# Pages by the time they are free, a searched order with GpSimd's rows behind accumulating DMAs, and f and g by seven from chunk 2 on

## The chip, the core and the metric

The kernel runs on one core of one Trainium2 chip. Its time is the device time of one execution in microseconds; the figure for a kernel is the median of its runs. A profiled execution also has a span, from the first to the last instruction that the profile shows.

The engines have short names in the profile: PE is TensorE (matmuls), PEld its weight loads, DVE is VectorE, ACT ScalarE, POOL GpSimd, SP the engine that issues most DMAs. Every instruction stands under the same line, L288, because one helper records and emits them all, so the text goes by the names of tiles.

## What is computed

One layer with a gated short convolution. `x` is 1024 x 1024 in float32, the inner width is 2048:

```python
def short_conv_mixer(u, w_in, conv_w, w_out):
    z, bg, cg, v = jnp.split(u @ w_in.astype(u.dtype), 4, axis=-1)
    y = bg * causal_dwconv(cg * v, conv_w) * jax.nn.silu(z)
    return y @ w_out.astype(u.dtype)

u = rms_norm(h, pre_norm[i])
m = short_conv_mixer(u, sc_w_in[j], sc_conv_w[j], sc_w_out[j])
h = h + rms_norm(m, post_norm[i])
```

## The kernel before

**Arithmetic.** Each float32 operand is split in a high and a low part, and each product is three matmuls (low x high, high x low, high x high). The input projection runs over 16 chunks `c` of 128 channels, each with two pairs `p = 2c` (the blocks CG and V) and `p = 2c + 1` (Z and BG). A pair is a 2 x 2 block product that is done with seven products, a to g, instead of eight; each is 12 matmuls of 512 columns. Some of the seven are themselves done by seven again, over a whole chunk: `by_seven(z, c)` (line 794) says so for z = b, f or g, from chunk DEEP, DEEP_F or DEEP_G on to the limits in LAST (b to chunk 15, f to 14, g to 13). A plain product costs 2 x 12 matmuls of 512 columns a chunk, one by seven 7 x 6 matmuls of 256 columns (`deep_product`, line 1432).

**What a product by seven needs.** Once for each z: `deep_subs` (line 1362) forms differences of the pages of u on GpSimd, eight rows of 256 columns, and `deep_split` (line 1375) splits four parts c', d', e', g' in high and low; with `by_bank` that is two casts and two copies to PSUM on ScalarE and one subtraction on VectorE for each part. g's source is read back from DRAM first (`load_ug`, line 1678). The table `UNDER` (line 1688) says after which product of which pair each of these is recorded. In each chunk besides: `deep_sums` (line 1399, four rows on GpSimd) and `deep_prep` (line 1414, the split of the weights), with `split_by_bank` (line 805) for several weights where f goes by seven.

**The output projection's weights.** They are summed in DRAM while the chunks run: `sums_plan` (line 979) and `out_sums` (line 995) issue plain copies into `t_d` on SP and then 16 accumulating DMAs on GpSimd's queue; `fetch_t` and `add_t` (lines 950 and 957) form other sums by loads, four GpSimd rows a time, and stores; `TODO` (line 1644) says at which pair. The stage after the chunks reads `t_d` in the order c, e, d, g (the tiles ru_c, ru_e, ru_d, ru_g).

**The order of the work.** From `plan.record()` on nothing is issued at once: each operation becomes an `Op` with a duration and its needs. `Plan.deadlines` (line 371) gives each a latest time, `boost` in PLAN moves single ones by hand-written amounts (by number of the operation), and `Plan.arrange` (line 424) runs the operations through a small model of the engines, which picks on each engine the ready one that is due first. TensorE's operations keep their order. The model knows that VectorE rows on SBUF operands and GpSimd rows take turns (`lock`, `own`, `grant`, `turn`). `take` (line 501) gives a GpSimd row to an idle VectorE. `sum_at` keeps accumulating DMAs apart. `emit` (line 631) then issues everything in that order, engine by engine.

**Pages.** Most SBUF tiles are pages of 512 floats a partition, 32 of them, made by `page` (line 691) under one tag `pg` with 32 buffers. `arrange` counts how many are free; which buffer a tile gets is left to the pool.

Of the kernel before, what the change touches and what calls it, by code (L numbers as in the profile page):

```python
# [18 lines left out]
PAGES = 32  # L19
DEEP = 2  # L20
DEEP_F = 3
DEEP_G = 4
LEAD = 7.0
PLAN = {
# [3 lines left out]
    "turns": 1,  # L28
    "hard": 2.0,
# [173 lines left out]

class Tile(View):

    __slots__ = ("pool", "args", "kw", "made", "parts", "writes", "reads", "left", "space", "key", "read", "summed", "n")

    def __init__(self, pool, shape, dtype, kw):
        ids = np.arange(int(np.prod(shape[1:]))).reshape(1, *shape[1:])
# [1892 lines left out]
```

## Time and profile before

| | |
|---|---|
| median of 3 runs | 776.25 us (776.20 to 776.41) |
| profiled execution | 776.59 us |
| its span | 774.8 us |
| mean granted TensorE clock | 0.998 |

The page gives the busy time of each engine in the span, then the chain of work that ended last. The views that the prediction quotes: waits (who waited for whom: us in total, times, longest), the timeline (start, length, engine, operation, tiles out<-in, shape, count, and in brackets the idle time before it and what ended it), groups of instructions (count, busy us, mean ns, idle before), and windows (stretch, length, then busy us and count of PE, PEld, DVE, ACT and POOL, the clock, the DMA share and GB/s).

### The profile page before, as it was taken

How to read it: one execution, taken by the hardware profiler on the slowest of the kernel's cores; microseconds unless marked ns; L12 is line 12 of the kernel's file. 1: busy time of each engine (PE TensorE's matmuls, PEld its weight loads, DVE VectorE, ACT ScalarE, POOL GpSimd, SP SyncE). 2: the span in 40 equal slices, each digit the busy share in tenths (PEclk: the TensorE clock that was granted, in tenths of full speed). 3: DMA queues.
4: the chain of work that ended last, by engine and by line, in shares of the span. 5: the costliest groups of instructions: out<-in, count | busy, mean ns of one | idle time of the engine just before them, and what ended most of it. 6: DMA issues, size and time to landing. Idle time of an engine off the chain costs nothing.

```text
span 774.8 us, 12631 instructions
## 1 busy us (share of the span) xinstructions
PE 763.8 (99%) x4266; PEld 668.0 (86%) x4266; DVE 669.9 (86%) x1009; ACT 451.2 (58%) x861; POOL 442.6 (57%) x397
## 2 busy tenths in 40 slices
PE   8999999999999999999999999999999999999996
PEld 7888888888988898988888888888888889889885
DVE  6899878786989898999899989797899899977993
ACT  7774456675755565756565656556553656564831
POOL 2518994558695859777788687565637100600321
PEclk9999999999999999999999999999999999999999
DMA  9222432354747575556667673724254998666842
GB/s 315 67 55 55 122 111 80 121 161 146 177 136 171 170 161 146 165 143 191 197 177 212 176 203 94 185 81 140 84 163 131 359 388 278 202 224 212 266 142 108
DMA packets 117136, 130.09 MB, mean 168 GB/s; under 512 B 7320, under 2 KB 74704, under 8 KB 116944
## 3 DMA queue, kind: packets, MB, share of 16 engines
q1 hardware_dynamic: 112560, 120.77, 48.4%
q0 software_dynamic: 4352, 8.39, 7.3%
q8 instruction: 33, 0.54, 0.3%
q14 instruction: 31, 0.25, 0.1%
q10 hardware_dynamic: 160, 0.14, 0.0%
HBM read 101.74 MB, written 44.30 MB: 188 GB/s over the span
## 4 chain that ended last, share of the span: by engine, by line
PE 97%; DVE 1%; issue 1%; DMA 1%; ACT 0%; POOL 0%; DVEq 0%; POOLq 0%; ACTq 0%
PE px L288 40%; PE pv L288 15%; PE po_x L288 11%; PE px2b L288 5%; PE px2f L288 3%; PE po_v L288 3%; PE pp L288 3%; PE px2g L288 3%; PE pv2b L288 2%; PE pv2f L288 2%; PE pf_x L288 1%; PE pb_x L288 1%; PE py2b L288 1%; PE py L288 1%; PE pv2g L288 1%
## 5 line engine op out<-in xcount | busy, mean ns | idle before, releaser
L288 PE MATMUL px<-u_d,wdh 128*128 128x512 f32 x248 | 76.7, 390 | 0.0
L288 PE MATMUL px<-u_a,wah 128*128 128x512 f32 x248 | 76.7, 390 | 0.0
L288 PE MATMUL pv<-u_e,weh 128*128 128x512 f32 x248 | 76.6, 390 | 0.0
L288 PE MATMUL px<-u_c,wch 128*128 128x512 f32 x248 | 76.6, 390 | 0.0
L288 ACT COPY beside<-raw 128x512 f32<-128x512 f32 x64 | 37.9, 592 | 37.5 <-DVE wal L288 13.3
L288 PEld LDWEIGHTS px<-u_d,wdh 128*128 128x128 f32 x248 | 46.6, 188 | 9.1
L288 PEld LDWEIGHTS px<-u_c,wch 128*128 128x128 f32 x248 | 46.7, 188 | 9.1
L288 PEld LDWEIGHTS pv<-u_e,weh 128*128 128x128 f32 x248 | 46.6, 188 | 9.0
L288 PEld LDWEIGHTS px<-u_a,wah 128*128 128x128 f32 x248 | 46.7, 188 | 8.9
L288 ACT COPY sna<-px 128x512 f32<-128x512 f32 x30 | 17.6, 586 | 60.4 <-PE px L288 55.6
L288 DVE SCALAR_TENSOR_TENSOR cv<-gpad,cw,cv 128x1024 f32<-128x1024 f32 x32 | 49.4, 1544 | 2.5 <-ACT cv L288 2.3
L288 PE MATMUL px<-u_d,wdl 128*128 128x512 f32 x124 | 48.8, 393 | 0.7 <-DVE wdl L288 0.7
L288 PE MATMUL px<-u_a,wal 128*128 128x512 f32 x124 | 48.6, 392 | 0.0
L288 PE MATMUL px<-u_c,wcl 128*128 128x512 f32 x124 | 48.5, 391 | 0.0
L288 PE MATMUL pv<-u_e,wel 128*128 128x512 f32 x124 | 48.5, 391 | 0.0
L288 POOL TENSOR_TENSOR sf<-raw,sc 128x512 f32<-128x512 f32 x27 | 41.2, 1524 | 10.8 <-issue 5.5
L288 POOL TENSOR_TENSOR raw<-raw,raw 128x512 f32<-128x512 f32 x31 | 45.2, 1459 | 3.5 <-DVE se L288 2.9
L288 POOL TENSOR_TENSOR sc<-se,raw 128x512 f32<-128x512 f32 x24 | 37.3, 1555 | 15.2 <-PE px L288 4.9
L288 POOL TENSOR_TENSOR se<-raw,raw 128x512 f32<-128x512 f32 x22 | 31.1, 1414 | 23.6 <-DVE sna L288 4.7
L288 POOL TENSOR_TENSOR rs_post<-ve_post,minus_half 128x1 f32<-128x1 f32 x7 | 4.9, 704 | 64.5 <-DVE ve_post L288 64.5
L288 ACT COPY snc<-px 128x512 f32<-128x512 f32 x31 | 18.0, 580 | 26.5 <-PE px L288 26.5
L288 POOL TENSOR_TENSOR sne<-snc,sne 128x512 f32<-128x512 f32 x10 | 13.5, 1346 | 33.7 <-ACT snc L288 31.9
(491 smaller groups left out, 2618.2 us busy)
## 6 DMA issues: line engine op xcount, KB each, us to landing
raw<-in_sc_w_in SPq DMA_DIRECT2D x128, 256.0 KB, 3.8
y_d<-cv SPq DMA_DIRECT2D x16, 512.0 KB, 2.7
s_d<-s SPq DMA_DIRECT2D x32, 256.0 KB, 3.2
t_d<-in_sc_w_out POOLq DMA_DIRECT2D x16, 512.0 KB, 7.9
t_d<-in_sc_w_out SPq DMA_DIRECT2D x16, 256.0 KB, 5.2
tb<-in_sc_w_out SPq DMA_DIRECT2D x16, 256.0 KB, 4.0
t_d<-t_d SPq DMA_DIRECT2D x16, 256.0 KB, 4.7
s<-y_d SPq DMA_DIRECT2D x16, 256.0 KB, 3.1
```

The costliest lines, as they stand in the source:

```text
L288: getattr(engine, name)(*(self.plain(a) for a in args), **{k: self.plain(a) for k, a in kw.items()})
```

## The change

Three things, and the numbers that go with them.

1. Pages are handed out by the run-through. `arrange` keeps a list of free page numbers; a new page takes the first, a page whose last use is over goes to the end. A tile then has its own tag, `pg` and the number, with one buffer. The tiles made before the recording take their numbers from a list, HEAD_SLOTS.
2. The run-through has a flag `kept`: after an accumulating DMA GpSimd keeps its turn on the shared operands as long as its next row is one of that sort, also ahead of a waiting VectorE row. Accumulating DMAs are kept apart by 11.0 instead of 15.0. The table of amounts in `boost` is another one, with 308 entries in place of 695.
3. DEEP_F goes from 3 to 2 and DEEP_G from 4 to 2: f goes by seven in chunk 2 too, g in chunks 2 and 3. UNDER is rewritten to suit. TODO follows DEEP_F, so `fetch_t` and `add_t` come two pairs earlier. The sums into t_d come in the order e, c, d, g from pair 15 on (e, d, c, g from pair 10 before), still 16 accumulating DMAs.

```diff
-DEEP_F = 3
-DEEP_G = 4
+DEEP_F = 2
+DEEP_G = 2
+HEAD_SLOTS = (
+    0, 23, 31, 30, 29, 28, 27, 26, 25, 24, 22, 21, 20, 1, 19, 18, 2, 17, 16, 15, 14, 3, 13, 12, 11, 10, 4, 7, 9, 8,
+    5, 6, 31, 29, 30, 28, 23, 0, 10, 11, 27, 26, 7, 4, 29, 15, 31, 16, 13, 3, 21, 22, 1, 20, 26, 27, 25, 30, 4, 7,
+)
...
+    "apart": 11.0,
...
     def get(self):
         if self.made is None:
-            self.made = self.pool.pool.tile(list(self.args[0]), self.args[1], **self.kw)
+            kw = self.kw
+            if kw["tag"] == "pg":
+                kw = dict(kw, tag=f"pg{self.slot}", bufs=1)
+            self.made = self.pool.pool.tile(list(self.args[0]), self.args[1], **kw)
...
+        held = [t.slot for k, ts in self.taken.items() if k[1] == "pg" for t in ts if t in self.users]
+        slots = self.slots = [n for n in range(PAGES) if n not in held]
...
-            if e == "vector" and not late and nxt is not None and nxt.lock:
+            more = nxt is not None and nxt.lock
+            self.kept = self.kept and (e == "vector" or more)
+            if more and (not late if e == "vector" else self.kept):
                 own[1] = e
...
+                        if x.key[1] == "pg":
+                            x.slot = slots.pop(0)
...
                     if e == "gpsimd" and op.order:
-                        self.sum_at = t + 15.0
+                        self.kept = True
+                        self.sum_at = t + p["apart"]
...
                     if left_of[x] == 0 and (x.read or x.key[1] == "cv"):
                         free[x.key] += 1
+                        if x.key[1] == "pg":
+                            slots.append(x.slot)
...
-    sums_plan(2 * DEEP_F + 4)
+    sums_plan({(n, h): 15 + 4 * "ecdg".index(n) + 2 * h for n in "ecdg" for h in (0, 1)})
...
-        ("d", 2 * DEEP): lambda: (deep_split("b", "c'", True), deep_split("b", "e'", True)),
-        ("f", 2 * DEEP): lambda: deep_subs("f", [0, 1]),
-        ("g", 2 * DEEP): lambda: deep_split("b", "d'", True),
-        ("e", 2 * DEEP + 1): lambda: deep_split("b", "g'", True),
-        ("d", 2 * DEEP_F): lambda: deep_split("f", "c'", True),
-        ("a", 2 * DEEP_F + 1): lambda: deep_split("f", "e'", True),
-        ("g", 2 * DEEP_F): lambda: deep_split("f", "d'", True),
-        ("c", 2 * DEEP_F + 1): lambda: deep_split("f", "g'", True),
-        ("e", 2 * DEEP_G - 2): load_ug,
-        ("e", 2 * DEEP_G - 1): lambda: deep_subs("g", [0]),
-        ("a", 2 * DEEP_G): lambda: deep_subs("g", [1]),
-        ("a", 2 * DEEP_G + 1): lambda: deep_split("g", "c'", True),
-        ("c", 2 * DEEP_G + 1): lambda: deep_split("g", "e'", True),
-        ("e", 2 * DEEP_G + 1): lambda: deep_split("g", "g'", True),
-        ("d", 2 * DEEP_G + 1): lambda: deep_split("g", "d'", True),
+        ("c", 2 * DEEP): lambda: (deep_split("b", "c'", True), deep_split("b", "e'", True)),
+        ("e", 2 * DEEP): lambda: (deep_split("b", "d'", True), deep_subs("f", [0, 1])),
+        ("d", 2 * DEEP): load_ug,
+        ("a", 2 * DEEP + 1): lambda: [deep_split("f", i, True) for i in ("c'", "e'", "d'")],
+        ("c", 2 * DEEP + 1): lambda: (deep_split("b", "g'", True), deep_split("f", "g'", True)),
+        ("e", 2 * DEEP + 1): lambda: deep_subs("g", [0, 1]),
+        ("d", 2 * DEEP + 1): lambda: [deep_split("g", i, True) for i in ("c'", "e'", "g'", "d'")],
```

More of the change, by code (lines that the diff above doesn't have):

```diff
@@ L204 @@
 class Tile(View):
-    __slots__ = ("pool", "args", "kw", "made", "parts", "writes", "reads", "left", "space", "key", "read", "summed", "n")
+    __slots__ = ("pool", "args", "kw", "made", "parts", "writes", "reads", "left", "space", "key", "read", "summed", "n", "slot")
     def __init__(self, pool, shape, dtype, kw):
@@ L215, in __init__ @@
         self.n = pool.plan.made
+        self.slot = None
     def get(self):
         if self.made is None:
-            self.made = self.pool.pool.tile(list(self.args[0]), self.args[1], **self.kw)
+            kw = self.kw
+            if kw["tag"] == "pg":
+                kw = dict(kw, tag=f"pg{self.slot}", bufs=1)
+            self.made = self.pool.pool.tile(list(self.args[0]), self.args[1], **kw)
         return self.made
@@ L231, in tile @@
         if not self.plan.recording:
+            if kw["tag"] == "pg":
+                t.slot = self.plan.slots.pop(0)
             t.get()
@@ L256, in __init__ @@
         self.nc, self.recording, self.ops, self.room, self.taken, self.made = nc, False, [], {}, {}, 0
+        self.slots = list(HEAD_SLOTS)
         for name in ("tensor", "vector", "scalar", "gpsimd", "sync"):
@@ L554, in arrange @@
                 note(held, ("held", op.engine, op, False))
-        self.shift, self.sum_at = 0.0, t
+        self.shift, self.sum_at, self.kept = 0.0, t, False
         self.stalls = []
@@ L570, in arrange @@
                     order.append(op)
-                    for x in op.news:
+                    for x in sorted(op.news, key=lambda x: x.n):
                         made.add(x)
                         free[x.key] -= 1
+                        if x.key[1] == "pg":
+                            x.slot = slots.pop(0)
                         owed[x.key].remove(op)
@@ L624, in arrange @@
                         note(ops[o].soft, None)
-                for x in op.tiles:
+                for x in sorted(op.tiles, key=lambda x: x.n):
                     left_of[x] -= 1
@@ L977, with sums_plan @@
     SUM_AT = {}
-    def sums_plan(p0):
-        order = [(n, h) for n in "edcg" for h in (0, 1)]
-        for j, (n, h) in enumerate(order):
+    def sums_plan(at):
+        for (n, h), p in at.items():
             js = slice(h * CQ, (h + 1) * CQ)
@@ L989, in sums_plan @@
             for b in range(CQ):
-                SUM_AT.setdefault(p0 + 2 * j - 1, []).append((to[n][:, b : b + 1], src[:, b : b + 1], False))
+                SUM_AT.setdefault(max(p - 1, 2), []).append((to[n][:, b : b + 1], src[:, b : b + 1], False))
             for k in (0, 1):
                 ks = slice(k * CQ // 2, (k + 1) * CQ // 2)
-                SUM_AT.setdefault(p0 + 2 * j + k, []).append((to[n][:, ks], more[:, ks], True))
+                SUM_AT.setdefault(p + k, []).append((to[n][:, ks], more[:, ks], True))
     def out_sums(p):
```

124 rows, old and new, of the table PLAN are left out of this document.

## The prediction

> **What bounds the kernel now.** I read the page first (its totals and chain), then the wait view of TensorE, then TensorE's own timeline around the waits that it names, and last the busy time of the other engines chunk by chunk.
>
> ```profile
> span 774.8 us, 12631 instructions
> PE 763.8 (99%) x4266; PEld 668.0 (86%) x4266; DVE 669.9 (86%) x1009; ACT 451.2 (58%) x861; POOL 442.6 (57%) x397
> PE 97%; DVE 1%; issue 1%; DMA 1%; ACT 0%; POOL 0%; DVEq 0%; POOLq 0%; ACTq 0%
> ```
> ```profile
> PE pw L288 <- DVE idle L288: 1.1, 1, 1.1
> PE pv2f L288 <- DVE dwf2l L288: 0.9, 1, 0.9
> PE px L288 <- DVE wdl L288: 0.7, 1, 0.7
> PE pk L288 <- DVE ve_pre L288: 0.6, 1, 0.6
> ```
>
> 97% of the chain that ends last is matmuls. The wait view of TensorE has six lines and 4.1 us in all; those on pw, pk and pp belong to the opening, in program order ahead of the recorded plan, and the diff leaves that order alone. So only two things can get shorter: the matmuls themselves, and the two waits on pv2f and px. No line of that view names a DMA: the loads are early enough.
>
> **Term 1, fewer matmul columns.** A product by seven takes 7 x 6 = 42 matmuls of 256 columns a chunk, a plain one 24 of 512. The change turns f of chunk 2 and g of chunks 2 and 3 into products by seven: three chunk-products. The price stands in the trace already, as the distance from the first matmul of product c in one chunk to the first in the next. Chunk 2 has only b by seven, chunk 3 b and f, chunk 6 all three:
>
> ```profile
> 100.01 0.39 PE L288 MATMUL px<-u_c,wcl 128*128 128x512 f32 x1
> 137.74 0.39 PE L288 MATMUL px<-u_c,wcl 128*128 128x512 f32 x1
> 175.07 0.39 PE L288 MATMUL px<-u_c,wcl 128*128 128x512 f32 x1
> 249.58 0.40 PE L288 MATMUL px<-u_c,wcl 128*128 128x512 f32 x1
> 286.50 0.40 PE L288 MATMUL px<-u_c,wcl 128*128 128x512 f32 x1
> ```
>
> 37.73 us, 37.33 us and 36.92 us: f by seven saves 0.40, g by seven 0.41. Three of them: 0.40 + 2 x 0.41 = **1.2 us less**. (Two of g's sub-products slide behind the next chunk's product c; they come back at g's other end.) This term hides behind nothing, since TensorE is the path.
>
> The Trainium skill, "TensorE: Matmul & The Clock Gate", section "Phases on the wall clock", gives the back-to-back gap as N/2.4 + 2.5 ns, 216 ns for 512 columns and so, as an estimate, 109 ns for 256; three chunk-products would then save 1.8 us, and the sum would be 0.6 us lower. The chunk lengths above say 0.40 and 0.41 for one, so the trace does not agree, and the sum goes by the trace.
>
> **Term 2, the two waits in chunk 5.** Here is TensorE at both, then VectorE and GpSimd in the microseconds before:
>
> ```profile
> 234.59 0.40 PE L288 MATMUL pv2b<-u_b,dwb2h 128*128 128x256 f32 x2
> 235.89 0.39 PE L288 MATMUL pv2f<-u_f,dwf2l 128*128 128x256 f32 x1 [0.90 <-DVE dwf2l L288]
> ...
> 237.87 0.28 PE L288 MATMUL px2f<-ufdl_deep,dwf2h 128*128 128x256 f32 x1
> 237.99 0.28 PE L288 MATMUL px2f<-ufdh_deep,dwf2h 128*128 128x256 f32 x1
> 239.00 0.50 PE L288 MATMUL px<-u_d,wdl 128*128 128x512 f32 x1 [0.74 <-DVE wdl L288]
> ```
> ```profile
> 231.99 3.25 DVE L288 TENSOR_TENSOR dwb<-raw,dwb 128x256 fp32r<-128x256 f32 x1
> 235.16 0.68 DVE L288 TENSOR_TENSOR dwf2l<-beside,dwf2h 128x512 fp32r<-128x512 f32 x1
> ```
> ```profile
> 230.41 1.15 POOL L288 DMA_DIRECT2D t_d<-in_sc_w_out  x1
> 231.16 1.17 POOL L288 TENSOR_TENSOR dsg<-dsg,raw 128x256 f32<-128x256 f32 x1
> 231.87 1.15 POOL L288 TENSOR_TENSOR dsg<-raw,raw 128x256 f32<-128x256 f32 x1
> 232.57 1.14 POOL L288 TENSOR_TENSOR dsg<-raw,dsg 128x256 f32<-128x256 f32 x1
> 233.56 1.38 POOL L288 TENSOR_TENSOR se<-raw,raw 128x512 f32<-128x512 f32 x1
> ```
>
> Matmuls of 256 columns start every 0.12 us here (237.87 to 237.99), so 1.06 us were lost at 235.89 and 0.89 at 239.00: 1.95 us, of which the wait view counts 1.64 since modelled ends overlap. The cause is in the rows below: GpSimd issues an accumulating DMA and then runs four rows back to back, and a VectorE subtraction with two SBUF inputs, queued at 231.99, ends only at 235.24, after 3.25 us. The order of before had no such rule: its run-through lets VectorE in between two GpSimd rows. The new run-through has it (the flag `kept`: GpSimd keeps its turn from the DMA on while its next row is of that kind), so it will put something harmless there. **1.95 us less**, at most; nothing, if the wait turns up elsewhere.
>
> The Trainium skill, "SBUF — State Buffer", section "Who interferes with whom", says that of a VectorE op with two SBUF inputs and a GpSimd op the second to issue blocks until the first finishes. By it the subtraction would have waited for one row and ended near 233.4 (an estimate), with no wait on TensorE; the 3.25 us over four rows differ, so the measurement decides.
>
> **Term 3, what the change adds.** The one-off work for products by seven (deep_subs, deep_split) was spread over chunks 1 to 5 and now falls in chunk 2. Busy time of chunks 1, 2, 3 and 6 (columns: PE, PEld, DVE, ACT, POOL, clock, DMA share, GB/s):
>
> ```profile
> 64.60:100.00 35.40, 35.40 (x157) 29.29 (x157) 31.60 (x32) 16.05 (x28) 32.90 (x23) 1.00 0.30 88
> 100.00:137.70 37.70, 37.70 (x187) 32.01 (x186) 28.40 (x42) 23.23 (x49) 26.63 (x22) 1.00 0.25 79
> 137.70:175.10 37.40, 37.40 (x206) 32.54 (x206) 28.62 (x47) 25.76 (x53) 20.12 (x20) 1.00 0.48 148
> 249.60:286.50 36.90, 36.90 (x224) 32.97 (x223) 33.15 (x50) 21.24 (x41) 27.65 (x25) 1.00 0.63 162
> ```
> ```profile
> L288 DVE TENSOR_TENSOR ugcl_deep<-beside,ugch_deep 128x512 fp32r<-128x512 f32 x1 | 0.7, 692 | 0.2 <-ACT beside L288 0.2
> L288 ACT COPY beside<-deepg 128x256 f32<-128x256 f32 x8 | 3.0, 376 | 1.2 <-DVE wdl L288 0.8 <-DVE dwb1l L288 0.3
> L288 ACT CAST uggh_deep<-deepg 128x256 fp32r<-128x256 f32 x2 | 0.8, 406 | 0.0
> L288 POOL TENSOR_TENSOR deepg<-deepg 128x256 f32<-128x256 f32 x4 | 2.9, 740 | 0.0
> L288 POOL TENSOR_TENSOR t<-t,tb 128x256 f32<-128x256 f32 x8 | 8.6, 1074 | 0.0
> ```
>
> One split is two casts and two copies on ScalarE (2 x 0.41 + 2 x 0.38 = 1.6 us) and one subtraction on VectorE (0.69). Twelve of them (b, f and g, four each) on top of a chunk like the sixth give VectorE 33.15 + 12 x 0.69 = 41.4 us and ScalarE 21.24 + 12 x 1.6 = 40.4 us in a chunk of 36.9. GpSimd has 27.65, less two accumulating DMAs (1.15 each) and four add_t rows (1.07 each in the last row) that chunk 2 hasn't, plus 16 rows of deep_subs at 0.74 for f and g: 33.2. So VectorE is 4.5 us over and ScalarE 3.5, **if nothing slides out**. It can slide: VectorE has 3.8 us free in chunk 1, and chunk 3, which loses its own f splits, has 37 - 33 = 4; ScalarE has 19 free in chunk 1. Deadlines limit the sliding: b's first splits are due in chunk 2, g's last two just after the first product of chunk 3. The price is therefore between 0 and 4.5 us, and where part of VectorE's time is waiting for GpSimd (the 3.25 us row is 0.41 of work), less than it looks.
>
> The accumulating DMAs stay 16, and move:
>
> ```profile
> L288 POOL DMA_DIRECT2D t_d<-in_sc_w_out x16: 1153/1171/1328, 189.0 to 485.0; - x16
> L288 SPq DMA_DIRECT2D ru_c<-t_d x8: 319/320/778, 626.4 to 635.2; - x8
> L288 SPq DMA_DIRECT2D ru_g<-t_d x8: 319/320/382, 707.6 to 729.5; - x8
> ```
>
> From pairs 10 to 25 they go to 15 to 30, five pairs of some 18.5 us: the last near 578 to 605. In the new order e, c, d, g the sum c is done by pair 22 (near 430, read at 626) and g by pair 30, read at 707, so nobody comes to wait for them. The add_t loads go two pairs earlier, load_ug (four loads on SP) to chunk 2, where the DMA share is 0.25. In chunks 7 to 10 add_t and sums coincide, before in 5 to 11: no loss visible, a small gain possible, both costed at 0.
>
> Pages: a tile now gets the page that has been free longest by the run-through, as a tag of one buffer, and its writer waits for that page's last reader. Behind a waiting fetch on SP stand the stores of cv and s and the copies into t_d, on ScalarE and VectorE the next splits. Before, SP already waits like that, and TensorE doesn't notice:
>
> ```profile
> SPq L288 <- ACT beside L288: 29.4, 8, 9.3
> ```
>
> Fetches lead by two pairs (37 us) and that longest wait is 9.3 us, so I take 0; a loss needs a page freed late on the chip where the plan has none to spare, and I bound it by the largest wait of TensorE now, 1.1 us, a gain by the 1.64 that are counted in term 2.
>
> What do I take for term 3? Between 0 and 4.5 I take 0.9, the nearest row that there is: the smaller of the two waits by which the old order missed the chip.
>
> **Sum.** The profiled execution took 776.59 us, 1.79 more than its span and 0.34 more than the median of 776.25. 776.59 - 1.2 - 1.95 + 0.9 = 774.3, and by the median **774.0 us**. A measurement tells 0.2% from no change, 1.55 us: faster is under 774.7, slower over 777.8.
>
> **Rivals.**
> - *The wait moves* (0.28): 16 accumulating DMAs still each hold VectorE back, and the packed chunk 2 costs one or two waits like those of before. Then only term 1 is left: 776.25 - 1.2 = 775.0, up to 777 where chunk 2 adds 2. For it: the DMAs are not fewer. Against: 15 of the 16 cost TensorE nothing already now.
> - *Chunk 2 saturates* (0.20, the other side): ScalarE and VectorE can't slide, g's and f's splits come late, TensorE waits on them between 120 and 145 us. It decides once more than 4.7 us of waits are left (1.2 + 1.95 + 1.55). Price: 4.5 from VectorE's sum and 0.9 elsewhere: 776.25 - 3.15 + 5.4 = 778.5. For it: both engines are over 36.9 by the sum. Against: 7.8 us free on VectorE on both sides.
> - *The run-through doesn't do what it says* is inside the first: if GpSimd's run of rows had another cause than the DMA, the 1.95 stay, 775.0.
> - *Nothing is left over* (part of the forecast): 776.25 - 3.15 = 773.1.
>
> **How the numbers follow.** Forecast 0.52: 773.1 to 774.7, likeliest 774.0. The range must reach into both rivals: 772.9 to 778.0 leaves out half of the saturated case and a little at the bottom. Faster 0.52, same 0.28, slower 0.20.
>
> **What would show it.** Right: 126 matmuls of 256 columns more and 72 of 512 fewer, 4320 in all; the distance between first matmuls of product c 36.9 us from chunk 3 on; no wait on dwf2l or wdl after an accumulating DMA, GpSimd's run of rows falling on VectorE rows that read PSUM. Wrong in term 3: lines in TensorE's wait view on ubgl, ufdl, ugcl, dwf or dwg between 120 and 145 us. Wrong in the pages: a wait on a DMA into raw, or a weight's cast waiting for a page's old reader. The forecast falls if those waits exceed 1.7 us together.

## The result and the profile after

The changed kernel takes 773.27 us (median of 6 runs, 772.79 to 774.06) against 776.37 us for the kernel before beside it: 3.1 us less, a ratio of 0.996 with a 95% interval of 0.9947 to 0.9972. The profiled execution took 772.83 us, its span is 771.0 us. The forecast was 774.0 us, faster.

The page's totals and chain, then the whole wait view of TensorE (who waited for whom: us in total, times, longest), both of the changed kernel, where the helper's line is L252:

```profile
span 771.0 us, 12816 instructions
PE 762.2 (99%) x4320; PEld 669.6 (87%) x4320; DVE 673.9 (87%) x1022; ACT 458.8 (60%) x880; POOL 462.2 (60%) x416
PE 98%; DVE 1%; DMA 0%; ACT 0%; POOL 0%; issue 0%; POOLq 0%; ACTq 0%
```
```profile
PE pw L252 <- DVE idle L252: 1.1, 1, 1.1
PE pp L252 <- ACT u_a L252: 0.5, 1, 0.5
PE pk L252 <- DVE xa L252: 0.3, 1, 0.3
```

The program has 4320 matmuls instead of 4266, as counted ahead. The lines on pv2f and px are gone and none came in their place: what is left of waits is the opening. Next, TensorE's timeline at the first matmul of product c in pairs 4, 6, 8, 12 and 14, the starts of chunks 2, 3, 4, 6 and 7:

```profile
99.55 0.39 PE L252 MATMUL px<-u_c,wcl 128*128 128x512 f32 x1
135.02 0.40 PE L252 MATMUL px<-u_c,wcl 128*128 128x512 f32 x1
171.94 0.40 PE L252 MATMUL px<-u_c,wcl 128*128 128x512 f32 x1
245.78 0.40 PE L252 MATMUL px<-u_c,wcl 128*128 128x512 f32 x1
282.70 0.40 PE L252 MATMUL px<-u_c,wcl 128*128 128x512 f32 x1
```

Chunk 3 now takes 36.92 us, as chunk 6 does. Chunk 2 takes 35.47, because two of g's sub-products slide behind the next product c, 1.4 us that the other end pays back.

To place the 3.1 us, one row of the view by tile is enough. It gives the first and the last start of the low part of product c, pair 1 to pair 31. First the kernel before, then the changed one:

```profile
L288 PE MATMUL px<-u_c,wcl x124: 389/389/396, 45.6 to 605.0; 128*128 128x512 f32 x124
```
```profile
L252 PE MATMUL px<-u_c,wcl x124: 389/389/396, 45.2 to 601.2; 128*128 128x512 f32 x124
```

This middle took 559.4 us and takes 556.0: **3.35 us less** by the starts to the nanosecond. All of it lies in chunks 2 to 5: from the first matmul of product c in chunk 2 to that in chunk 6 the kernel before took 149.57 us (100.01 to 249.58, shown in the prediction) and the changed one 146.23 (99.55 to 245.78). The opening ended 0.46 us earlier in this profile, and the stretch from the last such matmul to the end is the same within 0.02 us. The 0.46 can't be put down to the change: in the eleven profiles of this study the opening ends between 45.15 and 45.61 us, and two profiles of the changed kernel alone differ by 0.24.

One row more, of the accumulating DMAs in the changed kernel (first and last start):

```profile
L252 POOL DMA_DIRECT2D t_d<-in_sc_w_out x16: 1145/1176/1332, 276.2 to 556.7; - x16
```

The first of them now starts at 276.2 us instead of 189.0. So in chunk 5, where both waits were, there is no accumulating DMA any more.

### The profile page after: what moved, and what is told of

It reads as the page before. It is cut to its first block, busy times and chain, and to the rows that moved or that the text cites. A ratio compares the mean times of both kernels' runs of the same rounds, so it can differ in the third digit from the quotient of the medians.

```text
span 771.0 us, 12816 instructions
## 1 busy us (share of the span) xinstructions
PE 762.2 (99%) x4320; PEld 669.6 (87%) x4320; DVE 673.9 (87%) x1022; ACT 458.8 (60%) x880; POOL 462.2 (60%) x416
## 4 chain that ended last, share of the span: by engine, by line
PE 98%; DVE 1%; DMA 0%; ACT 0%; POOL 0%; issue 0%; POOLq 0%; ACTq 0%
PE px L252 39%; PE pv L252 15%; PE po_x L252 11%; PE px2b L252 5%; PE px2f L252 4%; PE px2g L252 3%; PE po_v L252 3%; PE pp L252 3%; PE pv2b L252 3%; PE pv2f L252 2%; PE pf_x L252 1%; PE pb_x L252 1%; PE py2b L252 1%; PE pv2g L252 1%; PE py L252 1%; PE pf_v L252 1%
## 5 line engine op out<-in xcount | busy, mean ns | idle before, releaser
L252 PE MATMUL px<-u_d,wdh 128*128 128x512 f32 x248 | 76.8, 390 | 0.0
L252 PE MATMUL px<-u_a,wah 128*128 128x512 f32 x248 | 76.7, 390 | 0.0
L252 PE MATMUL pv<-u_e,weh 128*128 128x512 f32 x248 | 76.7, 390 | 0.0
L252 PE MATMUL px<-u_c,wch 128*128 128x512 f32 x248 | 76.6, 390 | 0.0
L252 ACT COPY beside<-raw 128x512 f32<-128x512 f32 x67 | 39.6, 591 | 31.8 <-DVE wal L252 11.0
L252 PEld LDWEIGHTS px<-u_d,wdh 128*128 128x128 f32 x248 | 46.6, 188 | 9.1
L252 PEld LDWEIGHTS px<-u_c,wch 128*128 128x128 f32 x248 | 46.7, 188 | 9.0
L252 PEld LDWEIGHTS px<-u_a,wah 128*128 128x128 f32 x248 | 46.7, 188 | 8.9
L252 PEld LDWEIGHTS pv<-u_e,weh 128*128 128x128 f32 x248 | 46.6, 188 | 8.9
L252 DVE SCALAR_TENSOR_TENSOR cv<-gpad,cw,cv 128x1024 f32<-128x1024 f32 x32 | 49.7, 1554 | 3.4 <-ACT cv L252 3.3
L252 POOL TENSOR_TENSOR sf<-raw,sc 128x512 f32<-128x512 f32 x30 | 44.5, 1482 | 10.9 <-DVE sc L252 6.0
L252 PE MATMUL px<-u_d,wdl 128*128 128x512 f32 x124 | 48.7, 393 | 0.0
L252 PE MATMUL px<-u_a,wal 128*128 128x512 f32 x124 | 48.7, 393 | 0.0
L252 PE MATMUL px<-u_c,wcl 128*128 128x512 f32 x124 | 48.5, 392 | 0.0
L252 PE MATMUL pv<-u_e,wel 128*128 128x512 f32 x124 | 48.5, 391 | 0.0
L252 POOL TENSOR_TENSOR sc<-se,raw 128x512 f32<-128x512 f32 x25 | 36.5, 1460 | 19.0 <-DVE se L252 10.0
L252 ACT COPY sna<-px 128x512 f32<-128x512 f32 x30 | 17.6, 586 | 49.4 <-PE px L252 47.7
L252 POOL TENSOR_TENSOR raw<-raw,raw 128x512 f32<-128x512 f32 x31 | 44.8, 1446 | 3.3 <-DVE se L252 1.9
L252 POOL TENSOR_TENSOR rs_post<-ve_post,minus_half 128x1 f32<-128x1 f32 x7 | 5.4, 784 | 68.1 <-DVE ve_post L252 68.1
L252 POOL TENSOR_TENSOR se<-raw,raw 128x512 f32<-128x512 f32 x22 | 33.1, 1504 | 17.7 <-DMA raw<-in_sc_w_in 5.7
L252 DVE TENSOR_TENSOR wcl<-sc,wch 128x512 fp32r<-128x512 f32 x31 | 31.6, 1020 | 2.6 <-ACT wch L252 2.6
L252 DVE TENSOR_TENSOR sna<-px2b,sna 128x256 f32<-128x256 f32 x56 | 23.2, 413 | 11.9 <-PE px2b L252 11.9
```

Source lines behind the costliest of these rows:

```text
L252: getattr(engine, name)(*(self.plain(a) for a in args), **{k: self.plain(a) for k, a in kw.items()})
```

## The experiments

What there was to tell apart. My theory: the gain is matmul columns (1.2 us) and the two waits in chunk 5 (about 2 us); the waits came from GpSimd keeping its turn behind an accumulating DMA; which page a tile gets is worth nothing. The rivals: the waits have another cause; the pages carry the gain; chunk 2 is packed so full that only the searched amounts save it.

The kernel before, run beside each group of these, had medians of 776.52, 776.43 and 776.29 us; the ratios are to the one beside.

| kernel | median us | ratio to before, 95% interval |
|---|---|---|
| after_again (the changed kernel) | 773.37 | 0.9958, 0.9945 to 0.9970 |
| dma_later | 774.39 | 0.9975, 0.9965 to 0.9984 |
| before_slots | 776.00 | 0.9995, 0.9986 to 1.0004 |
| before_slots_later | 774.65 | 0.9982, 0.9973 to 0.9992 |
| no_kept | 776.24 | 0.9991, 0.9982 to 1.0000 |
| pages_last | 776.74 | 1.0004, 0.9995 to 1.0013 |
| pool_pages | 780.70 | 1.0051, 1.0038 to 1.0064 |
| no_boost | 780.20 | 1.0044, 1.0030 to 1.0058 |
| shallow_no_boost | 781.43 | 1.0060, 1.0041 to 1.0079 |

### The changed kernel again

> The changed kernel once more, to see how far its runs spread. Theory (1.2 us of matmuls and about 2 us of waits in chunk 5 are gone, nothing came in their place): 773.3 us, no wait of TensorE between the opening and the end. Rival (part of the 3.1 us is the opening, which was 0.46 us earlier in the changed kernel's profile): the opening differs from run to run by that much, and the distance from the first matmul of product c in pair 1 to the last in pair 31 stays 556.0 us.

773.37 us, and the middle 556.3 us. Two matmuls in chunk 14 start 0.2 and 0.1 us late, too little for the wait view; they make the 0.3 over the first profile. The rest agrees.

### One accumulating DMA issued later (dma_later)

```diff
         order = self.arrange(p)
+        op = next(o for o in order if o.n == 1708)
+        order.remove(op)
+        order.insert(next(k for k, o in enumerate(order) if o.n == 1492) + 1, op)
```

> The kernel before, with one change: the accumulating DMA at 230.41 us is issued some 9 us later on GpSimd's queue, behind five rows that followed it; nothing else moves. Theory (GpSimd's run of four rows behind that DMA held VectorE's row for 3.25 us and so made both waits in chunk 5): that row takes under 1.5 us, the waits on dwf2l and wdl are gone, 774.3 us (2 us less), unless the DMA holds another row where it now stands. Rival (GpSimd runs its rows back to back for another reason, or VectorE is late anyway): both waits stay, 776.3 us.

774.39 us, 2.1 us less than before. VectorE's timeline, and GpSimd's, of this kernel, where the prediction showed a row of 3.25 us:

```profile
231.85 0.42 DVE L288 TENSOR_TENSOR dwb<-raw,dwb 128x256 fp32r<-128x256 f32 x1
232.24 0.69 DVE L288 TENSOR_TENSOR dwf2l<-beside,dwf2h 128x512 fp32r<-128x512 f32 x1
232.85 0.41 DVE L288 TENSOR_TENSOR dwf<-sf,dwf 128x256 fp32r<-128x256 f32 x1
233.18 1.79 DVE L288 TENSOR_TENSOR dwg0l<-raw,dwg0h 128x512 fp32r<-128x512 f32 x1
234.90 0.68 DVE L288 TENSOR_TENSOR wdl<-beside,wdh 128x512 fp32r<-128x512 f32 x1
```
```profile
230.43 0.75 POOL L288 TENSOR_TENSOR dsg<-dsg,raw 128x256 f32<-128x256 f32 x1
231.25 0.74 POOL L288 TENSOR_TENSOR dsg<-raw,raw 128x256 f32<-128x256 f32 x1
231.95 0.92 POOL L288 TENSOR_TENSOR dsg<-raw,dsg 128x256 f32<-128x256 f32 x1
233.07 1.35 POOL L288 TENSOR_TENSOR se<-raw,raw 128x512 f32<-128x512 f32 x1 [0.20 <-DVE dwf2l L288]
...
239.66 1.17 POOL L288 DMA_DIRECT2D t_d<-in_sc_w_out  x1
```

The DMA now starts at 239.66, behind seven rows (the expectation counted five). The same GpSimd rows start within 0.8 us of where they did; only the DMA ahead of them is gone. Now VectorE comes in between them: dwb takes 0.42 us, dwf2l is done at 232.93 instead of 235.84, wdl at 235.58 instead of 238.95. Both waits of TensorE are gone, and the middle takes 557.25 us, **2.13 less**. All of that is in chunk 5, which takes 36.92 us instead of 39.05. So the DMA is the cause, shown by moving it alone. The rival falls. In the changed kernel, whose first accumulating DMA comes at 276.2 us, it is the new places of the sums that do the same. `kept` isn't needed for that: without it (the next run) chunk 5 takes 36.92 us as well. It can matter only where the DMAs now stand.

### The run-through without `kept` (no_kept)

```diff
                     if e == "gpsimd" and op.order:
-                        self.kept = True
                         self.sum_at = t + p["apart"]
```

> The changed kernel whose run-through does not know that GpSimd keeps its turn after an accumulating DMA; the amounts in boost are the same, so the order differs only from the first accumulating DMA on (276 us in the trace). Theory (this rule is what kept the waits of chunk 5 from coming back): one to three waits of TensorE of 0.5 to 2 us within 15 us of an accumulating DMA, 774.5 to 778 us. Rival (the rule does nothing, the searched amounts alone do it): within 0.2% of the changed kernel, 773.3 us.

776.24 us, 2.9 more than the changed kernel; the eleven runs spread from 773.65 to 776.83. Its wait view of TensorE has three lines beside those of the opening. These waits, at 402.5, 411.1 and 423.2 us, are all in chunk 10, which takes 40.14 us instead of 36.92. The timelines of VectorE and GpSimd show where it begins:

```profile
PE px2b L252 <- DVE dwb1l L252: 1.4, 1, 1.4
...
PE px L252 <- DVE wdl L252: 0.7, 1, 0.7
...
PE px L252 <- ACT snc L252: 0.3, 1, 0.3
```
```profile
391.76 4.73 DVE L252 TENSOR_TENSOR wel<-se,weh 128x512 fp32r<-128x512 f32 x1
```
```profile
391.50 1.18 POOL L252 DMA_DIRECT2D t_d<-in_sc_w_out  x1
392.26 1.75 POOL L252 TENSOR_TENSOR sne<-snc,sne 128x512 f32<-128x512 f32 x1
393.52 1.18 POOL L252 TENSOR_TENSOR tb<-tb 128x256 f32<-128x256 f32 x1
394.21 1.72 POOL L252 TENSOR_TENSOR se<-raw,raw 128x512 f32<-128x512 f32 x1
396.01 1.63 POOL L252 TENSOR_TENSOR raw<-raw,raw 128x512 f32<-128x512 f32 x1
```

A weight's low part, 0.68 us of work, is held for 4.73 us behind the run that follows the DMA. The changed kernel has a DMA at the same place. VectorE is held there too, on another row and for less; here se, GpSimd's third row behind the DMA, stands waiting for VectorE's gpad, and the run ends with that:

```profile
391.02 2.96 DVE L252 TENSOR_TENSOR gpad<-snc,sne 128x256 f32<-128x256 f32 x1
```
```profile
390.50 1.18 POOL L252 DMA_DIRECT2D t_d<-in_sc_w_out  x1
391.25 1.75 POOL L252 TENSOR_TENSOR sne<-snc,sne 128x512 f32<-128x512 f32 x1
392.51 1.18 POOL L252 TENSOR_TENSOR tb<-tb 128x256 f32<-128x256 f32 x1
394.06 1.29 POOL L252 TENSOR_TENSOR se<-raw,raw 128x512 f32<-128x512 f32 x1 [0.37 <-DVE gpad L252]
```

Nothing on TensorE waits for that. In the second profile of the changed kernel it is wel that is held there, for 3.22 us, and nothing waits for that either. So what differs is the length of the hold more than the row. The row dwb0l, behind the hold in both, starts at 393.91 us in the changed kernel and at 396.42 without the rule. Without the rule VectorE then stands idle only once before dwb1l, for 0.63 us. It comes to dwb1l 3.0 us late (410.36 against 407.40), and TensorE's wait of 1.4 us at 411 is for that row. The other two waits were not followed to a cause.

That does not make the 2.9 us the worth of the rule. The amounts in boost were made for an order with it, and this order differs from the first accumulating DMA on; a later run (pages_last, below) has the rule and loses time at the same three places.

### Pages: before_slots, before_slots_later, pool_pages, pages_last

The first takes the part on pages alone into the kernel before, with the diff of the change, and the second adds dma_later's edit to it.

> The kernel before with one part of the change alone: pages handed out by the run-through, in the order of before. Theory (pages matter only where the pool gives a page that is still in use; the kernel before has no such wait on TensorE, so there is nothing to gain): 776.4 us within 0.2%, the two waits of chunk 5 stay. Rival (handed-out pages are worth some 7 us in any order, as in the changed one): waits of TensorE differ in the middle and the time by more than 1.6 us, either way.

> The same, with the accumulating DMA at 230.41 us issued behind the five rows that followed it: everything that the change gives but the three chunk-products by seven, in the order of before. Theory (the gain is the sum of 1.2 us of matmuls and the waits of chunk 5): 774.3 us, no wait in the middle, and 1.1 us over the changed kernel. Rival (pages or other things give more): 773.5 us or less.

776.0 us, no difference that can be told, and 774.65 us. In the order of before the pages are worth nothing that the times can tell, as costed. The two waits did not stay quite as they were: in this profile the same DMA holds dwb for 2.58 us, and TensorE waits 0.2 for dwf2l and 1.0 for wdl. The second kernel has the pages and chunk 5 without its DMA, in the order of before, and no wait in the middle, which takes 557.3 us; the changed kernel's takes 556.0. The difference, **1.2 to 1.3 us, is the depth**, since the chunk lengths give it too: chunks 2 to 4 take 110.5 us before and 109.3 after. 774.65 to 773.37 says the same.

Then the other way round, the pool's pages in the changed order:

```diff
             kw = self.kw
-            if kw["tag"] == "pg":
-                kw = dict(kw, tag=f"pg{self.slot}", bufs=1)
             self.made = self.pool.pool.tile(list(self.args[0]), self.args[1], **kw)
```

> The changed kernel with pages handed out by the pool again, in the same order of the work. Theory (TensorE does not notice which page a tile gets): the same time as the changed kernel within 0.2%, 772.5 to 774.5 us, no new wait of TensorE in the middle. Rival (the handed-out pages carry part of the gain, because a writer no longer waits for a page that is still in use): slower by 1 us or more, with waits of TensorE on splits whose pages came late.

780.7 us: **7.3 us more**. My theory falls here. The wait views of ScalarE, VectorE and GpSimd in this kernel show whom they waited for, among DMAs:

```profile
ACT wah L250 <- DMA s_d<-s: 4.7, 1, 4.7
```
```profile
DVE dwg1l L250 <- DMA s_d<-s: 2.7, 1, 2.7
```
```profile
POOL dsg L250 <- DMA s_d<-s: 6.4, 2, 5.5
```

Splits of weights and sums of rows have nothing to do with s_d. They wait because their page holds an `s` that is still on its way to DRAM. In time, first the store on SP, then ScalarE, VectorE, GpSimd, VectorE again, then TensorE:

```profile
529.48 1.86 SPq L250 DMA_DIRECT2D s_d<-s  x1
```
```profile
537.00 0.62 ACT L250 CAST wah<-raw 128x512 fp32r<-128x512 f32 x1 [4.72 <-DMA s_d<-s]
```
```profile
538.14 0.69 DVE L250 TENSOR_TENSOR wal<-beside,wah 128x512 fp32r<-128x512 f32 x1 [4.40 <-ACT beside L250]
```
```profile
541.43 1.29 POOL L250 TENSOR_TENSOR sc<-se,raw 128x512 f32<-128x512 f32 x1 [11.96 <-DVE se L250]
```
```profile
544.44 1.76 DVE L250 TENSOR_TENSOR wcl<-sc,wch 128x512 fp32r<-128x512 f32 x1
```
```profile
546.35 0.47 PE L250 MATMUL px<-u_c,wcl 128*128 128x512 f32 x1 [1.46 <-ACT wah L250]
```

The store lands at 536.97 us by the trace, and the cast on ScalarE, which stood 4.72 us with everything behind it on that queue, starts at 537.00. VectorE stood 4.40 us for a copy behind that cast; its row se came late by that, GpSimd's sc waited for se, and wcl, made from sc, ended at 546.20, just before the matmul that reads it. (The view names wah, which ended 0.04 us later than wcl.) In all some 6 us of matmul starts were lost between 537 and 569 us. That the one delay led to the others is read from the order of the rows; the edit on pages as a whole is what the time shows. Not all of it is stores: 1.1 us is lost in chunk 1, before any wait for s_d, where VectorE's wcl waited 1.99 us for GpSimd's gpad, a row that it doesn't read. With handed-out pages none of these engines waits for a store to s_d, neither in the changed kernel nor in before_slots; the kernel before had four such waits, the longest of 2.6 us on VectorE, and TensorE felt none.

Is it the age of a free page that counts? One edit gives the page freed last instead of the oldest:

```diff
                         if x.key[1] == "pg":
-                            slots.append(x.slot)
+                            slots.insert(0, x.slot)
```

> The changed kernel with the same order of the work, but a page that comes free goes to the front of the list, so that a new tile gets the page freed last instead of the one that has been free longest. Theory (what counts is how long a page has been free when it is handed out: the pool's pages cost 7.4 us because tiles got pages whose store to s_d was still under way): many waits on old readers and on stores, TensorE waits in the middle, 780 us or more. Rival (only the pool's own bookkeeping costs; any page that the run-through counts as free is free on the chip as well): 773.3 us, no wait in the middle.

776.74 us: 3.4 more than the changed kernel, 4 less than with the pool's pages. ScalarE, VectorE and GpSimd don't wait for a store to s_d: the run-through calls a page free only when its store should have landed. TensorE's view has two lines beside those of the opening:

```profile
PE px2b L252 <- DVE dwb1l L252: 0.7, 1, 0.7
...
PE px L252 <- DVE wdl L252: 0.4, 2, 0.2
```

The middle takes 558.7 us, 2.65 more than in the first profile of the changed kernel, and 1.73 of that is in chunk 10. There the late starts are at 402.6, 410.5 and 422.2 us, the three places of no_kept, and again wel is held behind the DMA, for 4.38 us from 391.69.

So it matters that a page is free at all by the run-through, and which of the free pages is taken is worth 3.4 us in this order. That the age itself does it is not shown: most of the loss comes by way of the run behind one DMA, and how the page lengthens that run was not traced. Neither theory nor rival had it whole.

### No searched amounts: no_boost and shallow_no_boost

Both have `boost: {}`; the second also has DEEP_F = 3, DEEP_G = 4 and the table UNDER of before.

> The changed kernel with an empty boost table: the order as deadlines alone give it, not searched. Theory (chunk 2 is packed to the brim, and the searched amounts are what lets it fit): waits of TensorE of 1 to 5 us between 64 and 175 us, and others later, 780 to 795 us. Rival (chunk 2 had room all along): no wait between 64 and 175 us.

> The same without the depth: f from chunk 3 and g from chunk 4 on, the table UNDER and the pairs of add_t of before, empty boost table, handed-out pages, kept and the sums' new places as in the changed kernel. Theory (packing chunk 2 costs more than its matmuls save as long as the order is not searched): no wait between 64 and 175 us; faster than the run without boost and with the depth by its waits there less 1.2 us. Rival (depth is a gain with or without search): slower than it by 1.2 us, waits alike.

Between 64 and 175 us the run with the depth has one line in TensorE's wait view, the other none:

```profile
PE px2f L213 <- DVE dwf1l L213: 1.0, 1, 1.0
```

That wait is in chunk 3, at 156 us. By the first matmuls of product c the run with the depth loses 1.2 us in chunk 3 and 0.3 in chunk 2. So chunk 2, the packed one, holds without any searched amount, which is nearer to the rival than to my theory. What the three chunk-products save, such losses can just about eat (1.2 us against 1.5). Which of the two is faster stays open: 778.63 to 781.00 and 779.09 to 782.98 us in four runs each, which overlap; the profiled run was the slowest of the four with the depth and the fastest without. What the search is worth is plainer: the changed kernel is 7 us faster than its order without amounts.

## Why the prediction was right, and where not

- **Term 1, fewer columns: 1.2 us, measured 1.2 to 1.3.** By the lengths of chunks 2 to 4 (110.5 to 109.3 us), and by two kernels without waits, 557.3 against 556.0.
- **Term 2, the two waits: 1.95 us, measured 2.13.** The cause, GpSimd's run behind the DMA, is shown by moving one DMA. The size was short by 0.2, above the "at most" of the prediction, as the matmul after each waiting one also starts 0.1 us late, which the working didn't count. With term 1 it makes 3.35 us, the whole change of the middle. The means was another than forecast, though. The prediction gave the gain to `kept`, which would put something harmless behind the DMA, and costed the sums' new places at 0. In the changed kernel no accumulating DMA comes before 276.2 us, so it is the new places that took the waits out of chunk 5. In so far it is luck that the number came out.
- **Term 3, what is left over: 0.9 taken, 0 measured** in the first profile (0.3 in the second). This is the step that missed, by more than the 0.7 us between forecast and result. The 0.9 was a choice between 0 and 4.5 and not worked out. The sum behind the 4.5 put VectorE and ScalarE over the chunk, and was too high for VectorE. Busy time of chunks 1, 2, 3 of the changed kernel, and of two stretches as long as a chunk ahead of the first accumulating DMA:

```profile
64.20:99.60 35.40, 35.40 (x158) 29.33 (x157) 33.46 (x33) 20.92 (x40) 34.24 (x25) 1.00 0.28 83
99.60:135.00 35.40, 35.40 (x211) 31.51 (x210) 29.77 (x50) 29.62 (x73) 29.29 (x30) 1.00 0.40 119
135.00:171.90 36.90, 36.90 (x224) 32.96 (x223) 34.85 (x52) 23.99 (x47) 30.83 (x28) 1.00 0.35 112
...
174.00:211.00 37.00, 37.00 (x224) 33.05 (x223) 34.08 (x54) 22.30 (x43) 29.37 (x26) 1.00 0.37 118
211.00:248.00 37.00, 37.00 (x224) 33.06 (x223) 29.90 (x52) 21.46 (x42) 24.60 (x23) 1.00 0.35 111
```

  ScalarE has 74.5 us in the three chunks where the working makes it 16.05 + 40.4 + 21.2 = 77.7, so its work was counted about right, and it slid: 5 us more than before in chunk 1. VectorE has 98.1 us where the working makes it 31.6 + 41.4 + 33.2 = 106.2. The splits did not slide there: the rows of all twelve are in chunk 2. The base was wrong. Chunk 6 of the kernel before has two rows of the convolution (cv<-gpad,cw,cv, 3.5 us together) and four rows for g's parts (gs and px<-px,gs, 2.2 us); in the changed kernel chunk 2 has none of these six, as they come after the part of g that slides into chunk 3. That is 5.7 of the 8.1 us; the rest was not traced. (GpSimd's sum comes to 32.9 us by its own terms and not to 33.2, and 29.29 were measured; nothing rests on it.) What such a chunk takes varies besides: the two stretches at the end of the view, both ahead of the first accumulating DMA, differ by 4.2 us.
- **Pages at 0: right for the kernel before, wrong for the changed order.** "TensorE doesn't notice" was read from an order in which it didn't. In the changed one the pool's pages cost 7.3 us, far outside the bound of 1.1 us that I set from the longest wait of before. The forecast survives because the change had the handed-out pages, which is luck, as they were costed at nothing.
- **The rivals.** The wait didn't move: the DMAs still hold VectorE, up to 2.96 us in the first profile and 3.22 in the second, and TensorE doesn't wait. The sign that the runs would fall on VectorE rows that read PSUM did not come: the rows held, gpad and wel, have two SBUF operands. Chunk 2 did not saturate with the search; without it, it lost 0.3 us.
- **The sums' order and places:** TensorE never waits for t_d, as said. But the new places were not worth 0: they are what emptied chunk 5. The last of these DMAs starts at 556.7 us, earlier than the 578 to 605 worked out.

## What to carry to other kernels

When one engine is busy 99% of the time, look in its wait view for the few waits that are left, and follow each to the row that took several times its own length; moving the one instruction in front of it is a cheap experiment that settles the cause. An order laid out ahead and the buffers it runs in belong together: a buffer handed out while its store is in flight stops a whole queue; here the pool's choice of buffers cost nothing that the times can tell in one order and 7.3 us in the other. When an edit in a searched order costs time, look where it is lost before putting it down to the edit: two different edits lost it here at the same three matmuls. And when the busy time of one stretch is worked out from another, count the rows of both: the base here held six rows that the stretch did not have.

## What the runs showed of the hardware

- Behind an accumulating DMA, GpSimd's rows can hold a VectorE row with two SBUF operands over several of them: 3.25, 2.96 and 4.73 us for rows of 0.41, 0.41 and 0.68 us of work. With the first DMA moved away the same rows alternate, and the longest in that stretch was 1.79 us, 1.1 over its work, about one GpSimd row. It doesn't happen behind each of the 16: behind the other 15 of the kernel before no such row took more than 2.01 us, and behind those of the changed kernel's first profile 2.00. What makes the difference was not tested.
- That is the rule of the Trainium skill, "SBUF — State Buffer", section "Who interferes with whom" (the second to issue waits until the first finishes), in the stretch without the DMA; behind the DMA at these three places the trace does not agree with it, as the wait goes over two to four rows.
- A store of 256 KB to DRAM held its page for 7.5 us in one case, from its issue at 529.48 us to the start of the next writer at 537.00.
